# A two-layer attention, convolution and pooling backbone: which of the split operands of attention have 16 bits

## The chip, the cores and the metric

The kernel runs on one core of one Trainium2 chip. The metric is the device time in microseconds of one execution. The kernel before takes 3357.68 us (median of 3 runs, 3351.25 to 3362.43).

## The reference

Two groups of tokens go through two layers: 256 prompt tokens and 2048 sample tokens, each of width 1024. A layer normalizes its input, shifts and scales it, and projects it to queries (8 heads of 64), keys and values (2 heads of 64), gates, and inputs of a short convolution and of a pooling branch. Attention is the part that this case is about:

```
q = rmsnorm(q) * q_g;  k = rmsnorm(k) * k_g          # per head of 64
sample:  q, k = rotary(q), rotary(k);  k, v = [k, cached k], [v, cached v]   # 2048 + 256 keys
s = (q . k) * 64**-0.5
p = softmax(s)
attn = (p . v) * silu(z_a)
out = concat(attn, conv, pool) @ w_out
x = x + gate * out
```

All arrays are float32. The values, keys of the cache and query gains are drawn with a spread eight times the usual one.

## The kernel before, in words

To keep precision the kernel writes each operand of a product as a sum of a high part and a low part, and adds up the products that matter. Most parts have the 32-bit type fp32r, some are f16.

Each layer is two phases. **Phase A** (`phase_a`) loads the input, normalizes it, transposes it, and runs the input projection: per weight chunk, per block of 512 tokens, three products for each of 8 slices of the contraction (lines 477 to 479 and 638 to 640). What comes out goes to scratch arrays in device memory: queries in `q_unit` (high part `qH`, low part `qL`, and a rounded f16 copy `qB`), keys in `put_k` (`kH` and the f16 low part `kL`), values in `put_v` (`vS`, high and low part side by side, 64 + 64 columns). The stores are collected by `store` and issued on SP's queue by `stores` one step later.

**Phase B** (`phase_b`) is attention and the output projection. A unit is one head of one block of 512 queries (or two heads of the prompt's 256); there are 32 sample units of nine steps and four prompt units of one step in each layer, 292 steps. A step handles 256 keys as two tiles of 128:

- `qk` makes the scores of the two tiles in a PSUM tile of 128 x 1024. For each tile there are two products: line 1163 multiplies `KH` (the key's high part, twice, on the two halves of the partitions) with `T1` (the query's high and low part), and line 1164 multiplies `KL` (the key's low part) with `T2` (the rounded query). Row 64 of `KL` and `T2` carries the maximum that is taken off the scores.
- `expo` runs two exponentials on ScalarE: `P` in f32 (line 1173), and `ph`, the high part (line 1175). GpSimd subtracts `ph` from `P` and gives the f16 low part `pl` (line 1182, through the helper on line 183).
- `pv` multiplies values with probabilities: line 1209 takes the 128 columns of `V` (high and low part) with `ph`, two products a step. Line 1216 takes the values' high part `VH` (64 columns, f16, rounded from `V` by `round_v` on line 1048) with `pl`; these products wait in a list and run at the unit's end, 18 in a row, two by two on the two halves of the array's columns.
- `zsum` sums `P` over keys on VectorE (line 1195), in pieces; GpSimd adds the pieces up.
- `max_pieces` computes the scores of a later unit (line 1123) and VectorE reduces them to a maximum (line 1124), about two pieces a step; `max_a`, `max_b` turn the maximum into row 64 of `T2`.
- `outproj` puts some products of the output projection of the block before (lines 1336 to 1338) into each step. In the first of four blocks there is none.

Every engine works its instructions off in the order in which the program issues them, and the loop over steps (line 1605) is that order. At step 2 it calls `round_v` for both prompt heads and the first sample head group, so ScalarE holds those three casts ahead of step 2's exponentials; the casts of the second group come at step 22. `load_kv` loads keys and values on SP's queue and fills row 64 of `KL` (line 1043); its second part runs for the first group at the end of phase A, for the prompt at step 0 and for the second group at step 8. `load_q1` and `load_q2` load `T1` and `T2` some steps before a unit starts; PSUM holds two score tiles.

`outproj_tail` is the output projection of the last block. Its weights go into buffers that attention no longer needs: `half` uses the second group's key and value tiles, `later` and `final` use the tiles of `P` and (in `final`) of `ph`.

Of the kernel before, what the change touches and what calls it, by code (L numbers as in the profile page):

```python
# [22 lines left out]
NS = 2048  # L23
# [16 lines left out]
V_SCALE = 0.0625  # L40
M_SCALE = 256.0
# [55 lines left out]
def hybrid_step(ctx: ExitStack, tc: tile.TileContext, A, O):  # L97
# [25 lines left out]
    qB = [scratch(f"qB{p}", [128, NS], F16) for p in range(4)]  # L123
    qHp = [scratch(f"qHp{p}", [128, NP], F32) for p in range(4)]
    qLp = [scratch(f"qLp{p}", [128, NP], F32) for p in range(4)]
    qBp = [scratch(f"qBp{p}", [128, NP], F16) for p in range(4)]
# [3 lines left out]
    kLp = scratch("kLp", [128, NP], F16)  # L130
    vS = scratch("vS", [128, 18, 2, 128], F32)
    vSp = scratch("vSp", [128, 2, 2, 128], F32)
# [58 lines left out]
    def setup(tp, ptr):  # L191
# [14 lines left out]
        nc.vector.memset(lift, P_LOG2 * float(np.log(2.0)) * 8.0 / M_SCALE)  # L206
# [63 lines left out]
    def phase_a(l, xs_src, xp_src, nxt):  # L270


        with ExitStack() as st, ExitStack() as left:
# [261 lines left out]
            def q_unit(w, b, pair, c):  # L535
# [8 lines left out]
                def post(pair, q):  # L544
# [11 lines left out]
                    qb = w2("qb").bitcast(F16)[:, 0:512].rearrange("p (a n) -> p a n", a=2)  # L556
                    nc.scalar.copy(out=qb, in_=tr)
                    t0 = b.t0 + pair * 256
                    for hp in range(2):
                        dh, dl, db = (qHp, qLp, qBp) if b.prompt else (qH, qL, qB)  # L560
# [9 lines left out]
            def put_v(vsrc, dst):  # L570
                v = w2("vs", F32R)
# [7 lines left out]
            def put_k(k, dh, dl):  # L579
# [4 lines left out]
                lo = w1("kl").bitcast(F16)[:, 0:256]  # L584
                nc.scalar.copy(out=h[:, 0:256], in_=tr)
                nc.vector.tensor_tensor(out=lo, in0=tr, in1=h[:, 0:256], op=ALU.subtract)
                store(dh, h[:, 0:256])
                store(dl, lo)
# [415 lines left out]
    def phase_b(l, xs_src, xp_src, xs_dst, xp_dst, nxt):  # L1004
# [3 lines left out]
        with ExitStack() as st, ExitStack() as left:  # L1008
# [6 lines left out]
            def kv_tiles(prompt):  # L1015
                if prompt:
                    t = wk.tile([128, 4, 512], F32R, tag="cl", name="kvp", bufs=1)
                    vh = wk.tile([128, 2, 2, 64], F16, tag="VHp", name="VHp", bufs=1)
                    for g in range(2):
                        for a, v in zip(kvs[True], (t[:, g, 0:256], t[0:65, g, 256:384].bitcast(F16),  # L1020
                                                    t[:, 2 + g, 0:256].rearrange("p (t e) -> p t e", e=128), vh[:, g])):
                            a.append(v)
# [4 lines left out]
                low = p.tile([128, n + n // 2], F16, tag=f"L{g}", name="L")  # L1027
                for a, t in zip(kvs[False], (p.tile([128, n], F32R, tag=f"KH{g}", name="KH"), low[0:65, 0:n],
                                             p.tile([128, n // 128, 128], F32R, tag=f"V{g}", name="V"),
                                             low[:, n:].rearrange("p (t e) -> p t e", e=64))):  # L1030
                    a.append(t)

            def load_kv(prompt, g, first=True, second=True):
                KH, KL, V, VH = kvs[prompt]
# [6 lines left out]
                if second:  # L1041
                    nc.sync.dma_start(out=KL[g][0:64, 0:n], in_=sl[r, :])
# [7 lines left out]
            kvs = {False: ([], [], [], []), True: ([], [], [], [])}  # L1050
# [10 lines left out]
            def make_unit(prompt, blk, h):  # L1061
# [5 lines left out]
                u.KH, u.KL, u.V, u.VH = kvs[prompt]  # L1067
# [22 lines left out]
            def load_q2(u):  # L1090
                sb = qBp if u.prompt else qB
                u.T2 = lk.tile([65, 512], F16, tag="T2", name="T2", bufs=3)
                for r, ts, c in q_parts(u):
                    nc.sync.dma_start(out=u.T2[0:64, c], in_=sb[u.pair][r, ts])
# [55 lines left out]
            def max_b(u):  # L1150
                ps = borrow["ps"]() if borrow else pmx.tile([128, 512], F32, tag="mx", name="mxb")
                nc.tensor.matmul(out=ps, lhsT=ones_r, rhs=u.dg)
                nc.scalar.activation(out=u.T2[64:65, :], in_=ps[64:65, :], func=AF.Identity, bias=lift[64:65, :],
                                     scale=1.0 / M_SCALE)

# [565 lines left out]
```

## Time and profile before

| | us |
|---|---|
| median of 3 runs | 3357.68 |
| the profiled execution | 3371.42 |
| its span, first to last instruction | 3369.6 |
| busy: PE / VectorE / GpSimd / ScalarE | 3138.9 / 2446.6 / 2125.9 / 1845.8 |

The trace belongs to the profiled execution, which is 13.7 us longer than the median. Phase A of the two layers lies at about 0 to 715 us and 1640 to 2320 us of the span, phase B at about 720 to 1640 us and 2330 to 3370 us. TensorE's work is shown as two engines: PE for the products and PEld for loading their stationary operands. The recorded time of one product is longer than the distance to the next one, since products overlap in the array; the distance between starts says what a product costs.

### The profile page before, as it was taken

Reading aid. Unit: us, or ns where it says so; the run is one execution under the profiler, and the core shown is the slowest. Engines: PE = TensorE matmul, PEld = TensorE weight load, DVE = VectorE, ACT = ScalarE, POOL = GpSimd, SP = SyncE. Lnnn points to the kernel's source line nnn. Section 1 sums busy time; section 2 is a strip of 40 time slices with the busy share of each in tenths; the row PEclk is TensorE's granted clock in tenths of the full one; section 3 lists DMA queues with packets and bytes.
Section 4 is the critical chain, followed back from the end, with each engine's and each line's share of the span. In section 5 each row is a group of like instructions: output and inputs, shape, how many; then the busy total and the mean of one; then the engine's idle time right before and its main releaser. Section 6 shows DMA issues by size and latency. Waiting matters only on the chain. (4 is left out here: it accounts for less than half of the span.)

```text
span 3369.6 us, 48369 instructions
## 1 busy us (share of the span) xinstructions
PE 3138.9 (93%) x17818; PEld 2369.1 (70%) x17818; DVE 2446.6 (73%) x3860; ACT 1845.8 (55%) x2654; POOL 2125.9 (63%) x1192
## 2 busy tenths in 40 slices
PE   6899999988999999999999999999889899998998
PEld 4788888754566666667788787887456566665667
DVE  6546474458888888888466536635898988999885
ACT  3232333248777777777433323323787677776772
POOL 3325352238998898888453435322798888887883
PEclk9999999999999999999999999999899999999999
DMA  7246645350241323133523555334113324232245
GB/s 240 79 151 197 222 131 160 128 130 23 89 144 49 97 74 97 56 114 118 203 85 117 180 181 167 113 103 114 50 54 119 123 60 128 74 111 85 76 138 197
DMA packets 377380, 402.66 MB, mean 119 GB/s; under 512 B 21940, under 2 KB 329144, under 8 KB 376632
## 3 DMA queue, kind: packets, MB, share of 16 engines
q1 hardware_dynamic: 377144, 399.56, 38.3%
q8 instruction: 142, 2.33, 0.3%
q14 instruction: 94, 0.77, 0.1%
HBM read 278.09 MB, written 121.39 MB: 119 GB/s over the span
## 5 line engine op out<-in xcount | busy, mean ns | idle before, releaser
L183 POOL TENSOR_TENSOR pl<-P,ph 128x1024 f16<-128x1024 f32 (+2 forms) x594 | 1401.4, 2379 | 242.3 <-ACT ph L1175 223.2
L1124 DVE TENSOR_REDUCE mr<-mx 128x1 f32<-128x512 f32 x1024 | 693.9, 683 | 214.5 <-PE mx L1123 210.2
L1173 ACT ACTIVATE P<-st 128x1024 f32<-128x1024 f32 x576 | 635.1, 1103 | 324.9 <-PE st L1164 313.8
L1195 DVE TENSOR_REDUCE Z<-P 128x152 f32<-128x912 f32 (+2 forms) x576 | 695.4, 1208 | 13.5 <-ACT P L1173 12.6
L1175 ACT ACTIVATE ph<-st 128x1024 fp32r<-128x1024 f32 x584 | 592.2, 1014 | 0.0
L1123 PE MATMUL mx<-KH,T 128*128 128x512 f32 x1024 | 507.7, 496 | 56.8 <-DVE mr L1124 38.1
L1163 PE MATMUL st<-T,KH 128*128 128x512 f32 x1152 | 506.0, 498 | 9.6 <-ACT ph L1175 9.6
L638 PE MATMUL rest<-xh,wh 128*128 128x512 f32 (+1 forms) x1280 | 486.1, 380 | 1.9 <-ACT wh L428 1.5
L640 PE MATMUL rest<-xh,wl 128*128 128x512 f32 (+1 forms) x1280 | 476.7, 372 | 6.7 <-DVE wl L430 4.9
L639 PE MATMUL rest<-xl,wh 128*128 128x512 f32 (+1 forms) x1280 | 476.8, 372 | 0.8 <-POOL xl L183 0.8
L1164 PE MATMUL st<-T,L 65*128 65x512 f16 x1152 | 459.4, 399 | 0.0
L1209 PE MATMUL pv<-ph,V 128*128 128x512 f32 x1152 | 385.5, 416 | 11.5 <-DVE o L1228 11.5
L1164 PEld LDWEIGHTS <-L 65*128 65x128 f16 x1152 | 113.7, 99 | 302.7 <-issue 301.8
L1123 PEld LDWEIGHTS mx<-KH,T 128*128 128x128 f32 x1024 | 200.3, 196 | 169.7 <-DVE mr L1124 104.8
L430 POOL TENSOR_TENSOR wl<-wf,wh 128x512 fp32r<-128x512 f32 x88 | 121.9, 1386 | 300.5 <-ACT wh L428 285.1
L640 PEld LDWEIGHTS rest<-xh,wl 128*128 128x128 f32 x1280 | 244.1, 191 | 50.5 <-DVE wl L430 5.9
L638 PEld LDWEIGHTS rest<-xh,wh 128*128 128x128 f32 x1280 | 244.9, 191 | 47.2 <-issue 6.3
L639 PEld LDWEIGHTS rest<-xl,wh 128*128 128x128 f32 x1280 | 244.8, 191 | 38.5 <-POOL xl L183 1.2
L477 PE MATMUL qkv<-wh,xh 128*128 128x256 f32 x864 | 252.2, 292 | 3.1 <-ACT wh L428 3.1
L478 PE MATMUL qkv<-wl,xh 128*128 128x256 f32 x864 | 248.8, 288 | 5.3 <-DVE wl L430 2.8
L1163 PEld LDWEIGHTS st<-T,KH 128*128 128x128 f32 x1152 | 229.8, 200 | 26.4 <-ACT ph L1175 12.7
L479 PE MATMUL qkv<-wh,xl 128*128 128x256 f32 x864 | 247.9, 287 | 0.0
(231 smaller groups left out, 5833.0 us busy)
## 6 DMA issues: line engine op xcount, KB each, us to landing
wo<-woH SPq DMA_DIRECT2D x68, 512.0 KB
wo<-woL SPq DMA_DIRECT2D x68, 512.0 KB
wf<-in_w_in SPq DMA_DIRECT2D x50, 512.0 KB
wa<-in_w_ada SPq DMA_DIRECT2D x24, 1024.0 KB
wf<-in_w_in SPq DMA_DIRECT2D x19, 1024.0 KB
woH<-wgh SPq DMA_DIRECT2D x64, 256.0 KB
woL<-wgl SPq DMA_DIRECT2D x64, 256.0 KB
xS<-ox SPq DMA_DIRECT2D x24, 512.0 KB
```

The lines of the kernel that those rows point to most:

```text
L183: nc.gpsimd.tensor_tensor(out=out, in0=a, in1=b, op=op)
L638: nc.tensor.matmul(out=ps[:, 0:b.n], lhsT=wh[:, k, ms], rhs=b.h[:, k, :], start=(k == 0), stop=False)
L639: nc.tensor.matmul(out=ps[:, 0:b.n], lhsT=wh[:, k, ms], rhs=b.l[:, k, :], start=False, stop=False)
L640: nc.tensor.matmul(out=ps[:, 0:b.n], lhsT=wl[:, k, ms], rhs=b.h[:, k, :], start=False, stop=(k == KD - 1))
L1123: nc.tensor.matmul(out=ps, lhsT=u.T1[:, q * 128:(q + 1) * 128], rhs=u.KH[u.g][:, c * 512:(c + 1) * 512])
L1124: nc.vector.reduce_max(out=mr[:, q, c:c + 1], in_=ps, axis=AX.X)
L1163: nc.tensor.matmul(out=ps[:, i, :], lhsT=u.KH[u.g][:, kt], rhs=u.T1, start=True, stop=False)
L1164: nc.tensor.matmul(out=ps[:, i, :], lhsT=u.KL[u.g][0:65, kt], rhs=u.T2, start=False, stop=True)
L1173: nc.scalar.activation(out=P, in_=ps, func=AF.Exp, scale=0.125)
L1175: nc.scalar.activation(out=ph, in_=ps, func=AF.Exp, scale=0.125)
L1195: nc.vector.tensor_reduce(out=z[:, c], in_=u.P[grp][:, 0:ns, c, :].rearrange("p s n t -> p n s t"), axis=AX.XY, op=ALU.add)
L1209: nc.tensor.matmul(out=u.po, lhsT=u.V[u.g][:, 2 * j + i, :], rhs=ph[:, i, :], start=(j == 0 and i == 0), stop=False)
```

## The change

The low score product (line 1164) gets 32-bit operands: `kL` and its tile are fp32r, and `T2` is loaded from `qH` instead of from the rounded copy. The copy `qB`, its cast and its stores are gone. The product of values and probabilities (line 1209) gets 16-bit operands: `vS` holds an f16 high part and an f16 low part, and `ph` is f16. The values' high part that line 1216 uses is now the first 64 columns of `V`, so `VH` and `round_v` are gone. The two scale factors that kept f16 in range are 1 now (`V_SCALE`) or gone (`M_SCALE`). Row 64 of `KL` is filled by a copy of a one instead of a memset. In the tail, `final` can't use the smaller `ph` tiles any more, and half of one weight part is loaded by `later`.

```
-V_SCALE = 0.0625
-M_SCALE = 256.0
+V_SCALE = 1.0
...
-    qB = [scratch(f"qB{p}", [128, NS], F16) for p in range(4)]
-    kL = scratch("kL", [128, NS + NC], F16)
+    kL = scratch("kL", [128, NS + NC], F32)
-    vS = scratch("vS", [128, 18, 2, 128], F32)
+    vS = scratch("vS", [128, 18, 2, 128], F16)
...
-                    qb = w2("qb").bitcast(F16)[:, 0:512].rearrange("p (a n) -> p a n", a=2)
-                    nc.scalar.copy(out=qb, in_=tr)
...
-                        store(db[2 * c + hp][:, t0:t0 + 256], qb[:, hp, :])
...
-                v = w2("vs", F32R)
+                v = w2("vs").bitcast(F16)[:, 0:512]
...
-                lo = w1("kl").bitcast(F16)[:, 0:256]
+                lo = w1("kl", F32R)
...
-                low = p.tile([128, n + n // 2], F16, tag=f"L{g}", name="L")
-                for a, t in zip(kvs[False], (p.tile([128, n], F32R, tag=f"KH{g}", name="KH"), low[0:65, 0:n],
-                                             p.tile([128, n // 128, 128], F32R, tag=f"V{g}", name="V"),
-                                             low[:, n:].rearrange("p (t e) -> p t e", e=64))):
+                for a, t in zip(kvs[False], (p.tile([128, n], F32R, tag=f"KH{g}", name="KH"),
+                                             p.tile([65, n], F32R, tag=f"KL{g}", name="KL"),
+                                             p.tile([128, n // 128, 128], F16, tag=f"V{g}", name="V"))):
...
-                    nc.vector.memset(KL[g][64:65, 0:n], M_SCALE)
-                    load(V[g], sv[:, :, g, :])
-
-            def round_v(prompt, g):
-                V, VH = kvs[prompt][2:]
-                nc.scalar.copy(out=VH[g], in_=V[g][:, :, 0:64])
...
+                    nc.vector.tensor_copy(out=KL[g][64:65, 0:n], in_=ones1[64:65, 0:1].to_broadcast([1, n]))
+                    nc.sync.dma_start(out=V[g], in_=sv[:, :, g, :])
...
-                u.T2 = lk.tile([65, 512], F16, tag="T2", name="T2", bufs=3)
+                u.T2 = lk.tile([65, 512], F32R, tag="T2", name="T2", bufs=3)
...
-                ph = wk.tile([128, 2, 512], F32R, tag="ph", name="ph", bufs=LAG)
+                ph = wk.tile([128, 2, 512], F16, tag="ph", name="ph", bufs=LAG)
...
-                        nc.tensor.matmul(out=u.po[64 * i:64 * i + 64], lhsT=u.VH[u.g][:, 2 * j + i, :], rhs=pl[:, i, :],
+                        nc.tensor.matmul(out=u.po[64 * i:64 * i + 64], lhsT=u.V[u.g][:, 2 * j + i, 0:64], rhs=pl[:, i, :],
...
                 def later():
-                    load_w(2, 1, wk.tile([128, KD, 256], F32R, tag="P", name="wt", bufs=2), 0)
+                    w = wk.tile([128, 12, 256], F32R, tag="P", name="wt", bufs=2)
+                    load_w(2, 1, w[:, 0:8], 0)
+                    load_w(3, 1, w[:, 8:12], 4)
                     load_x(1, "ox", D, 2)
...
                 def final():
-                    for k0 in (4, 0):
-                        load_w(3, 1, wk.tile([128, 4, 256], F32R, tag="ph", name="wt", bufs=LAG), k0)
-                    load_w(3, 0, wk.tile([128, KD, 256], F32R, tag="P", name="wt", bufs=2), 0)
+                    w = wk.tile([128, 12, 256], F32R, tag="P", name="wt", bufs=2)
+                    load_w(3, 1, w[:, 8:12], 0)
+                    load_w(3, 0, w[:, 0:8], 0)
...
-                if s == 2:
-                    for g in range(2):
-                        round_v(True, g)
-                    round_v(False, 0)
...
-                if s == PR['rv1']:
-                    round_v(False, 1)
```

## Rows read from the trace of the kernel before

**Rows 1.** Stretches: us, busy us of each engine (instructions), granted clock, DMA share, GB/s.

```profile
100.00:715.00 615.00, 588.55 (x3545) 504.97 (x3544) 326.28 (x660) 181.31 (x335) 212.28 (x178) 0.98 0.50 155
720.00:1000.00 280.00, 251.39 (x1253) 154.82 (x1251) 240.88 (x325) 220.38 (x289) 241.92 (x114) 0.97 0.31 89
1000.00:1600.00 600.00, 583.60 (x3287) 404.57 (x3286) 516.24 (x698) 439.37 (x537) 527.03 (x243) 0.99 0.29 88
2600.00:3280.00 680.00, 637.89 (x3483) 433.93 (x3482) 615.38 (x814) 489.41 (x670) 564.08 (x260) 0.97 0.33 100
727.00:736.00 9.00, 5.68 (x18) 3.50 (x16) 5.67 (x7) 7.11 (x8) 6.48 (x4) 0.62 0.64 168
```

**Rows 2.** Waits of PE, 2600 to 3280 us: total us, times, longest us.

```profile
PE mx L1123 <- DVE mr L1124: 22.7, 38, 2.6
```

**Rows 3.** Timeline of ScalarE and PE, start of layer 0's attention: start, us, engine, instruction.

```profile
727.39 0.30 ACT L1048 CAST VHp<-kvp 128x128 f16<-128x128 f32 x1 [1.90 <-DMA kvp<-vSp]
728.65 1.06 ACT L1173 ACTIVATE P<-st 128x1024 f32<-128x1024 f32 x1
...
726.02 0.39 PE L1164 MATMUL st<-T,L 65*128 65x512 f16 x1
730.66 0.80 PE L1163 MATMUL st<-T,KH 128*128 128x512 f32 x1 [3.32 <-ACT ph L1175]
```

**Rows 4.** Timeline of SP's queue and PE there: the prompt's last query load.

```profile
727.35 0.59 SPq L180 DMA_DIRECT2D T<-qLp  x1
732.23 0.99 PE L1130 MATMUL mx<-kvp,T 128*128 128x256 f32 x2
```

**Rows 5.** Timeline of PE in phase A: the first and the last of 27 products.

```profile
299.98 0.40 PE L638 MATMUL rest<-xh,wh 128*128 128x512 f32 x1
305.88 0.39 PE L640 MATMUL rest<-xh,wl 128*128 128x512 f32 x1
```

**Rows 6.** Timeline of PE in one dense step of attention.

```profile
1030.72 0.63 PE L1209 MATMUL pv<-ph,V 128*128 128x512 f32 x2
1031.42 0.39 PE L1163 MATMUL st<-T,KH 128*128 128x512 f32 x1
1031.65 0.39 PE L1164 MATMUL st<-T,L 65*128 65x512 f16 x1
1032.12 0.39 PE L1164 MATMUL st<-T,L 65*128 65x512 f16 x1
```

**Rows 7.** Timeline of PE at a unit's end, and the durations of line 1216 (min/median/max).

```profile
1019.21 0.63 PE L1209 MATMUL pv<-ph,V 128*128 128x512 f32 x2
1019.77 2.13 PE L1216 MATMUL pv<-pl,L 128*64 128x512 f16 x18
...
L1216 PE MATMUL pv<-pl,L x1152: 376/379/637, 754.2 to 3313.8; 128*64 128x512 f16 x192
```

**Rows 8.** Timeline of PEld (weight loads) in that dense step.

```profile
1031.65 0.10 PEld L1164 LDWEIGHTS <-L 65*128 65x128 f16 x1 [0.27 <-issue]
```

**Rows 9.** Groups of GpSimd by form: busy us, mean ns | idle before and releasers.

```profile
L183 POOL TENSOR_TENSOR pl<-P,ph 128x1024 f16<-128x1024 f32 x558 | 1361.8, 2459 | 237.3 <-ACT ph L1175 218.3 <-PE mx L1123 13.6 <-PE pv L1209 1.7
L183 POOL TENSOR_TENSOR Z<-Z 128x512 f32<-128x512 f32 x128 | 166.7, 1303 | 99.9 <-DVE Z L1195 86.4 <-PE st L1164 7.2 <-PE pv L1216 2.5
L183 POOL TENSOR_TENSOR ml<-po,mh 128x1032 fp32r<-128x1032 f32 x4 | 11.9, 2972 | 25.4 <-ACT mh L656 25.4
```

**Rows 10.** Groups of ScalarE: the casts of the queries.

```profile
L557 ACT CAST qb<-trq 128x512 f16<-128x512 f32 x36 | 21.1, 585 | 141.8 <-DVE ql L555 132.7 <-POOL ra L183 9.1
L554 ACT CAST qh<-trq 128x512 fp32r<-128x512 f32 x36 | 20.8, 577 | 12.1 <-DVE sq L517 4.9 <-DVE nt_v L156 2.5 <-DMA qB<-qb 2.4
```

**Rows 11.** Groups of VectorE: the memset of row 64, and two products of 512 columns.

```profile
L1043 DVE MEMSET L<- 1x2304 f16 x4 | 7.9, 1978 | 8.9 <-DMA mH<-mh 7.3 <-issue 1.6
L1279 DVE TENSOR_TENSOR mixl<-o,mixh 128x512 fp32r<-128x512 f32 (+1 forms) x40 | 77.8, 1946 | 3.4 <-ACT mixh L1274 3.4
L1267 DVE TENSOR_TENSOR o<-o,rlb 128x512 f32<-128x512 f32 (+1 forms) x40 | 25.0, 624 | 10.5 <-PE rlb L1266 10.4
```

More of the change, by code (lines that the diff above doesn't have):

```diff
@@ L205, in setup @@
         nc.vector.memset(vones_h, V_SCALE)
-        nc.vector.memset(lift, P_LOG2 * float(np.log(2.0)) * 8.0 / M_SCALE)
+        nc.vector.memset(lift, P_LOG2 * float(np.log(2.0)) * 8.0)
         nc.vector.memset(sT, 0.0)
@@ L1017, in kv_tiles @@
                     t = wk.tile([128, 4, 512], F32R, tag="cl", name="kvp", bufs=1)
-                    vh = wk.tile([128, 2, 2, 64], F16, tag="VHp", name="VHp", bufs=1)
                     for g in range(2):
-                        for a, v in zip(kvs[True], (t[:, g, 0:256], t[0:65, g, 256:384].bitcast(F16),
-                                                    t[:, 2 + g, 0:256].rearrange("p (t e) -> p t e", e=128), vh[:, g])):
+                        for a, v in zip(kvs[True], (t[:, g, 0:256], t[0:65, g, 256:512], t[:, 2 + g, 0:128]
+                                                    .bitcast(F16).rearrange("p (t e) -> p t e", e=128))):
                             a.append(v)
@@ L1041, in load_kv @@
                 if second:
-                    nc.sync.dma_start(out=KL[g][0:64, 0:n], in_=sl[r, :])
-                    nc.vector.memset(KL[g][64:65, 0:n], M_SCALE)
-                    load(V[g], sv[:, :, g, :])
-            def round_v(prompt, g):
-                V, VH = kvs[prompt][2:]
-                nc.scalar.copy(out=VH[g], in_=V[g][:, :, 0:64])
-            kvs = {False: ([], [], [], []), True: ([], [], [], [])}
+                    load(KL[g][0:64, 0:n], sl[r, :])
+                    nc.vector.tensor_copy(out=KL[g][64:65, 0:n], in_=ones1[64:65, 0:1].to_broadcast([1, n]))
+                    nc.sync.dma_start(out=V[g], in_=sv[:, :, g, :])
+            kvs = {False: ([], [], []), True: ([], [], [])}
             kv_tiles(False)
@@ L1066, in make_unit @@
                 u.nst = 1 if prompt else 9
-                u.KH, u.KL, u.V, u.VH = kvs[prompt]
+                u.KH, u.KL, u.V = kvs[prompt]
                 u.g = h // 4
@@ L1090, in load_q2 @@
             def load_q2(u):
-                sb = qBp if u.prompt else qB
-                u.T2 = lk.tile([65, 512], F16, tag="T2", name="T2", bufs=3)
+                sh = qHp if u.prompt else qH
+                u.T2 = lk.tile([65, 512], F32R, tag="T2", name="T2", bufs=3)
                 for r, ts, c in q_parts(u):
-                    nc.sync.dma_start(out=u.T2[0:64, c], in_=sb[u.pair][r, ts])
+                    load(u.T2[0:64, c], sh[u.pair][r, ts])
             def load_z(u):
@@ L1152, in max_b @@
                 nc.tensor.matmul(out=ps, lhsT=ones_r, rhs=u.dg)
-                nc.scalar.activation(out=u.T2[64:65, :], in_=ps[64:65, :], func=AF.Identity, bias=lift[64:65, :],
-                                     scale=1.0 / M_SCALE)
+                nc.scalar.activation(out=u.T2[64:65, :], in_=ps[64:65, :], func=AF.Identity, bias=lift[64:65, :])
             GRP = 3
```

15 lines of the change are left out of this document (7 added, 8 removed).

## The prediction

> **What bounds the kernel now.** I read the stretches first, then the waits of PE, then the timelines of PE, PEld and ScalarE, and last the groups by form. In phase A TensorE is the bound: PE is busy 588.55 of 615 us, ScalarE 181.31 [rows 1]. In attention's blocks 2 to 4 of layer 0 PE is busy 583.60 of 600 us, with GpSimd at 527.03 and VectorE at 516.24; in the same blocks of layer 1 it is 637.89 of 680, with VectorE at 615.38 [rows 1], and there PE waits 22.7 us for VectorE's maxima alone [rows 2]. In the first block (720 to 1000 us) nobody is full: PE 251.39 of 280, GpSimd 241.92, VectorE 240.88 [rows 1]. So the reader is to see a kernel in which PE ends last, with two engines 5 to 12 points behind it: a saving on PE is passed on nearly whole in layer 0's dense blocks, about half in layer 1's, a third in first blocks. Weighted by steps (216, 216 and 144 of 576 sample steps, shares 0.9, 0.5, 0.3) I pass on 0.6.
>
> **Part 1, the casts of `round_v`.** At step 2 of layer 0, ScalarE has its three casts ahead of the exponentials and sits 1.90 us idle for the second prompt value to land. The scores of step 2 were through at about 726.02 + 0.39 = 726.41, but `P` starts at 728.65: 2.24 us late. PE then waits 3.32 us [rows 3], and after that pause the granted clock is down: 0.62 on average over 727 to 736 us, against 0.99 in the dense blocks [rows 1], so it is at the lower of its two levels, 1.2 GHz, for much of that time. Without the casts the pause shrinks from 3.7 to about 1.5 us. If the clock still falls, the gain is 2.24 us; if it doesn't, up to half of the 5.3 us from 730.66 to 736 is saved too, and it is about 5. What is late next is the prompt's query: its last load is issued until 727.94, and the maximum of line 1130 needs it, at 732.23 today and about 730.0 then [rows 4]. The load has 2 us to land in; so there is room for 2.2 us and little more, and I take 3 per layer. Layer 1 starts in the same way, so 6 us, between 4 and 10. The cast at step 22 lies beside a ScalarE that is busy 439.37 of 600 us [rows 1]: nothing.
>
> **Part 2, the products on PE.** One fp32r product of 512 columns costs (305.88 - 299.98) / 26 = 227 ns from start to start in phase A [rows 5]. In attention it costs more: from `pv` at 1030.72 to `st` at 1031.42 lie three, 233 ns each [rows 6]. A pair of line 1164 and line 1163 costs 1032.12 - 1031.65 = 470 ns by the printed digits, and the f16 product follows the fp32r one by 230 [rows 6]: f16 behind fp32r costs about what fp32r costs, 225 to 240. Only f16 behind f16 is cheaper: the 18 of line 1216 are nine pairs side by side, and (2130 - 379) / 8 = 219 ns lie between pairs [rows 7].
>
> - `pv`: two fp32r (466 ns) become two f16: the first behind fp32r, about 228, the second behind f16, 219, less what the first pair's start costs in that figure, 216. That is 22 ns less a step, 576 x 22 = 12.7 us. Bounds: 0 if f16 is no cheaper here, 2 x 17 x 576 = 20 us if both run at 216.
> - `KL`: an f16 between fp32r becomes fp32r. From -6 ns (phase A's 227 instead of 233) to +10; I take +6, for two a step 12 x 576 = 6.9 us more (-7 to +12). Its weight load, 0.10 us now [rows 8], gets longer, but fp32r loads run under the product before, as phase A's cadence of 227 shows.
> - the unit's end: from `pv` at 1019.21 to line 1216 at 1019.77 are 560 ns, where two products cost 466; some 95 ns are lost at the change from fp32r to f16 of 64 columns [rows 7]. If the type makes that gap it goes (64 units x 0.1 = 6.4 us); if the change to half columns makes it, it stays. I take half, 3.2.
>
> Together 12.7 - 6.9 + 3.2 = 9.0 us, passed on at 0.6: 5.4 us (-7 to +18 before passing on).
>
> The Trainium skill, "TensorE: Matmul & The Clock Gate" (Back-to-back issue gap), gives N / 2.4 + 2.5 ns for a warm product whatever its type: 216 ns at 512. By that rule alone part 2 is nothing, and the sum below would be 7.5 us. The f16 rows agree (219 with the first pair in it), the fp32r rows don't (227 and 233), and the measurement decides; the rule is in the second rival.
>
> **Part 3, the engines beside PE.** `ph` as f16: ScalarE's two casts from one PSUM tile take 585 ns to f16 and 577 to fp32r [rows 10], so the 584 exponentials gain or lose some 16 ns each, under 10 us on an engine that is a quarter idle: 0. GpSimd's subtraction then reads one 16-bit operand, which no row shows. What it writes makes no difference (2459 ns for 1024 columns to f16, 1303 for 512 to f32, so a slope per column that fits both), and I take 2.46 us unchanged; nearest rows on either side are 1303 and 2972 ns [rows 9]. It has slack: GpSimd is busy 88% of the dense blocks, so up to some 13% more hides, and a faster one gains nothing while PE is the bound.
>
> **Part 4, phase A.** 36 casts `qb` (21.1 us) and 72 stores go. The cast also makes ScalarE sit 141.8 us, mostly for VectorE's subtraction of the same tile [rows 10], with weight casts behind it. But PE waits little there: 615 - 588.55 = 26.5 us in layer 0, most of it for VectorE. I take 3 us, 0 to 10. Fewer stores help SP's queue, which nothing on PE waits for there.
>
> **Part 5, loads and row 64.** `T2` and `KL` double in bytes, `V` halves; `T2` is loaded five steps (15 us) before its unit, like `T1`, whose loads have the size `T2` gets. Nothing. The copy into row 64 replaces a memset of 1978 ns [rows 11]; from 0 to as much again. VectorE operations with two SBUF operands suffer beside GpSimd: 1946 ns against 624 for one with a PSUM operand and the same 512 columns [rows 11]. If the copy suffers so too it waits for one subtraction, up to 2.46 us, at two long copies in phase B and four short ones. I take 1.5 us more in all (0 to 10).
>
> The Trainium skill, "SBUF — State Buffer" (SBUF: two separate sides), says that VectorE's two-port operations, fp32 copies from SBUF to SBUF among them, and GpSimd's instructions lock each other out for a whole instruction. By it each copy in phase B pays what I have as the upper end; without it, nothing. The rows on the two products agree with a lock; none shows a copy.
>
> The tail moves 0.5 MB from `final` to `later`, before its use; the tail's waits are on `cl`, loaded earlier. Nothing, 2 us either way.
>
> **Sum**, against the profiled execution's 3371.42 us (span 3369.6 and 1.8 around it): -6 - 5.4 - 3 + 1.5 = -12.9, so 3358.5. The median of the runs shown is 13.7 us under that execution; the same change from 3357.68 gives 3345.
>
> **Rivals.**
> 1. The gain is absorbed (chance 0.31). PE's term is nothing, by the skill's rule or because `KL` gives back what `pv` saves; the other terms are -6 - 3 + 1.5 = -7.5, or 3350, and with VectorE and GpSimd taking more, up to 3357. For it: every f16 product between fp32r ones costs as much as fp32r. Against it: PE's own pause at step 2 is not hidden by anything.
> 2. The other side: the values' weight load shows (0.09). An f16 load starts only when the product before it is through (line 1164's load starts at 1031.65, with its product; its idle is put down to "issue") [rows 8], and at the unit's end 95 ns are lost in just such a load [rows 7]. If `V` with 128 rows behaves like that one and not like line 1164's, each step pays 0.1 us in front of `pv`: (100 + 12) x 576 = 64.5, passed on 0.6, 39 us, less 6 and 3, plus 1.5: +31, or 3389. It decides from about 40 ns a step. Against it: line 1164's load has as many columns, 128, and shows no gap.
> 3. GpSimd's mixed subtraction is slower (0.05). At 2972 ns, nine per unit add 4.6 us to the 9 x 2.459 + 2 x 1.303 + 0.65 = 25.4 us of GpSimd per unit, which makes 30. A unit takes about 29 (527.03 / 25.4 = 20.7 units in the 600 us [rows 1]), so GpSimd would be full at +1 us a unit, and with some idle time left +1.4: 64 x 1.4 = 90, or 3450. It decides from 13%. No row of a 16-bit operand speaks for it.
>
> **How the numbers follow.** The forecast has 0.55. A measurement of this kernel can't tell a change under 0.3%, 10 us, from none. Faster by more: 0.55, the forecast with its better half of bounds; within: 0.31; slower: 0.14, rivals 2 and 3. All good ends together (-10, 0.9 x 18, -10) make -36, 3321, and I go to 3320; upwards the bounds of the forecast and part of rival 2 reach 3366. The forecast's own range is 3325 to 3350.
>
> **What would show it.** Right: no casts of line 1048 and a pause of PE under 2 us at step 2; starts of line 1209's pairs nearer to 445 than 466 ns; line 1164 at 230 to 240; GpSimd's subtraction within 2% of 2.46 us. Wrong: a gap ahead of line 1209 in each step, a subtraction over 2.7 us, a unit's length that stays at its old value, a new wait on row 64 or on the prompt's loads.

## The result: 44 us faster, three times the forecast and more

The changed kernel takes 3311.22 us (median of 4 runs, 3305.09 to 3318.36), the one before 3355.03 (3351.25 to 3362.43): a ratio of 0.9864 with the 95% interval 0.9838 to 0.9889, where 3345 was forecast and 3320 the lower end. The profiled executions have spans of 3311.0 and 3369.6 us.

The page of the changed kernel, busy time by engine: PE works 21.6 us less than before, GpSimd 153.7, ScalarE 24.2.

```profile
PE 3117.3 (94%) x17818; PEld 2457.1 (74%) x17818; DVE 2439.7 (74%) x3860; ACT 1821.6 (55%) x2610; POOL 1972.2 (60%) x1192
```

Its stretches, in the columns of [rows 1] (the second to fourth are the first block, the dense blocks of layer 0 and those of layer 1):

```profile
100.00:711.00 611.00, 589.93 (x3557) 506.08 (x3556) 331.64 (x661) 172.64 (x319) 213.40 (x179) 0.98 0.49 151
720.00:1000.00 280.00, 256.68 (x1298) 175.06 (x1296) 246.74 (x334) 221.99 (x294) 226.94 (x118) 0.97 0.33 96
1000.00:1600.00 600.00, 586.52 (x3360) 442.59 (x3360) 516.69 (x699) 449.17 (x548) 485.69 (x250) 1.00 0.30 88
2600.00:3250.00 650.00, 613.24 (x3370) 454.69 (x3368) 575.17 (x779) 472.78 (x645) 492.66 (x258) 0.97 0.34 103
```

GpSimd in the dense blocks fell from 527.03 to 485.69 us of 600. Its subtraction is why, and with it VectorE's `mixl` fell ([rows 9] and [rows 11]); the copy into row 64 costs about what the memset did, and PE's waits for VectorE's maxima in layer 1's dense blocks are halved, 22.7 us [rows 2] to 12.1 (over the whole traces they fall from 38.1 to 33.7 only):

```profile
L180 POOL TENSOR_TENSOR pl<-P,ph 128x1024 f16<-128x1024 f32 x558 | 1211.6, 2183 | 319.0 <-ACT ph L1162 295.7 <-PE mx L1111 11.6 <-PE st L1151 4.7
...
L1266 DVE TENSOR_TENSOR mixl<-o,mixh 128x512 fp32r<-128x512 f32 (+1 forms) x40 | 68.7, 1717 | 3.0 <-ACT mixh L1261 3.0
L1035 DVE CAST KL<-ones 1x2304 fp32r<-1x2304 f32 x4 | 8.2, 2044 | 6.9 <-DMA mL<-ml 6.8
...
PE mx L1111 <- DVE mr L1112: 12.1, 20, 1.9
```

Two timelines answer to [rows 3] and [rows 7]. Where ScalarE's casts stood, `P` starts 2.73 us after the one ahead of it, and between 720 and 733 us PE waits 0.43 us at the longest, for a query's load. At a unit's end the low products start 0.54 us after the last pair, 0.56 before: the pair is shorter, the gap of some 0.1 us at the change to half columns is still there.

```profile
724.97 1.17 ACT L1160 ACTIVATE P<-st 128x1024 f32<-128x1024 f32 x1
727.70 1.09 ACT L1160 ACTIVATE P<-st 128x1024 f32<-128x1024 f32 x1 [0.66 <-PE st L1151]
...
726.25 0.48 PE L1118 MATMUL mx<-kvp,T 128*128 128x256 f32 x2 [0.43 <-DMA T<-qLp]
...
1036.57 0.61 PE L1196 MATMUL pv<-ph,V 128*128 128x512 f16 x2
1037.11 0.84 PE L1203 MATMUL pv<-pl,V 128*64 128x512 f16 x6
```

The first of a unit's low products marks its end, and these 64 marks cut every trace into the same six stages (us; "units" are 32 in a layer, the first eight follow the projections):

| kernel (span) | to first mark | layer 0 attention | to layer 1's first mark | layer 1, eight units | layer 1, the other 23 | after the last |
|---|---|---|---|---|---|---|
| before (3369.6) | 754.2 | 890.7 | 726.9 | 243.4 | 695.8 | 58.6 |
| c_before (3361.9) | 755.8 | 887.2 | 724.1 | 242.0 | 694.7 | 58.1 |
| changed (3311.0) | 744.7 | 879.3 | 703.6 | 235.9 | 688.2 | 59.3 |
| a_qb (3345.4) | 747.0 | 891.8 | 720.5 | 240.1 | 687.3 | 58.8 |
| b_qbfirst (3353.7) | 750.9 | 891.6 | 713.1 | 243.4 | 696.5 | 58.2 |
| b_split (3325.3) | 756.6 | 880.7 | 727.3 | 238.1 | 664.4 | 58.3 |
| a_split (3284.8) | 737.9 | 882.4 | 701.8 | 241.4 | 661.7 | 59.6 |
| a_pool (3280.2) | 735.5 | 874.7 | 702.1 | 243.9 | 664.8 | 59.2 |

The largest drop, some 20 us, lies in layer 1's projections; the rest is spread over attention and the start. The first column also varies by some 10 us between kernels that do the same there. Each row is one execution: that of a_qb lies 15 us above its median, that of b_qbfirst 14.

### The profile page after: what moved, and what is told of

Read it like the earlier page. It is cut to its first block, busy times and chain, and to the rows that moved or that the text cites. A ratio compares the mean times of both kernels' runs of the same rounds, so it can differ in the third digit from the quotient of the medians.

```text
span 3311.0 us, 48199 instructions
## 1 busy us (share of the span) xinstructions
PE 3117.3 (94%) x17818; PEld 2457.1 (74%) x17818; DVE 2439.7 (74%) x3860; ACT 1821.6 (55%) x2610; POOL 1972.2 (60%) x1192
## 5 line engine op out<-in xcount | busy, mean ns | idle before, releaser
L180 POOL TENSOR_TENSOR pl<-P,ph 128x1024 f16<-128x1024 f32 (+2 forms) x594 | 1247.5, 2113 | 325.3 <-ACT ph L1162 301.4
L1162 ACT ACTIVATE ph<-st 128x1024 f16<-128x1024 f32 x584 | 591.8, 1013 | 0.0
L1111 PE MATMUL mx<-KH,T 128*128 128x512 f32 x1024 | 494.1, 483 | 46.7 <-DVE mr L1112 33.7
L1150 PE MATMUL st<-T,KH 128*128 128x512 f32 x1152 | 466.8, 405 | 3.1 <-ACT ph L1162 3.1
L1151 PE MATMUL st<-T,KL 65*128 65x512 f32 x1152 | 464.2, 403 | 0.0
L1196 PE MATMUL pv<-ph,V 128*128 128x512 f16 x1152 | 357.8, 393 | 8.8 <-DVE o L1215 6.1
L1151 PEld LDWEIGHTS st<-T,KL 65*128 65x128 f32 x1152 | 221.8, 193 | 48.8
L1150 PEld LDWEIGHTS st<-T,KH 128*128 128x128 f32 x1152 | 222.6, 193 | 42.9 <-ACT ph L1162 6.1
L180 POOL TENSOR_TENSOR Z<-Z 128x512 f32<-128x512 f32 x128 | 166.5, 1300 | 136.6 <-DVE Z L1182 110.9
```

The costliest lines, as they stand in the source:

```text
L180: nc.gpsimd.tensor_tensor(out=out, in0=a, in1=b, op=op)
L1111: nc.tensor.matmul(out=ps, lhsT=u.T1[:, q * 128:(q + 1) * 128], rhs=u.KH[u.g][:, c * 512:(c + 1) * 512])
L1150: nc.tensor.matmul(out=ps[:, i, :], lhsT=u.KH[u.g][:, kt], rhs=u.T1, start=True, stop=False)
L1151: nc.tensor.matmul(out=ps[:, i, :], lhsT=u.KL[u.g][0:65, kt], rhs=u.T2, start=False, stop=True)
L1162: nc.scalar.activation(out=ph, in_=ps, func=AF.Exp, scale=0.125)
L1196: nc.tensor.matmul(out=u.po, lhsT=u.V[u.g][:, 2 * j + i, :], rhs=ph[:, i, :], start=(j == 0 and i == 0), stop=False)
```

## The experiments

Each label beginning with "a" edits the changed kernel, with "b" the one before. All ratios are to the kernel before, with their 95% intervals.

**c_before** has no edit.

> The kernel before, unchanged, for a second trace of it: same, 3355 us within 0.3%. Theory 1 (ScalarE's in-order stalls) expects PE's pauses in the query units of layer 1's phase A and at step 2 to be there again, about 17 us and 2 x 5.6 us; if they are an accident of the first trace, they are gone here and theory 1 falls.

3357.23 us, 0.9996 (0.9975 to 1.0017). The long first units and the 724.1 us of layer 1's projections come back, so they belong to the kernel.

**a_qb: the query cast alone put back.**

```
+                    qb = w2("qb").bitcast(F16)[:, 0:512].rearrange("p (a n) -> p a n", a=2)
+                    nc.scalar.copy(out=qb, in_=tr)
...
+                        store(db[2 * c + hp][:, t0:t0 + 256], qb[:, hp, :])
```

> The kernel after with the f16 cast of the queries and its stores put back; nothing reads the copy. Theory 1: most of phase A's gain goes, +15 to +20 us on 3311, so 3326 to 3331. Rival (my prediction's part 4, the cast is hidden beside PE): +3 us, 3314. Rival 2 (GpSimd's faster subtraction is the gain): +0 to 3.

3332.45 us, 0.9921 (0.9890 to 0.9952): 21 us over the changed kernel (19, give or take 13, by the two intervals). The two traces are 34 us apart, 17 of them in layer 1's projections (703.6 to 720.5) and 12 in layer 0's attention. By the medians nearly half of the gain is this cast.

**b_qbfirst: the cast kept, and issued ahead of VectorE's subtraction.**

```
-                    nc.vector.tensor_tensor(out=lv, in0=tr, in1=hv, op=ALU.subtract)
                     ...
                     nc.scalar.copy(out=qb, in_=tr)
+                    nc.vector.tensor_tensor(out=lv, in0=tr, in1=hv, op=ALU.subtract)
```

> The kernel before with two lines of the projection exchanged: ScalarE's 16-bit cast of the query is issued ahead of VectorE's subtraction that makes the 32-bit low part; no work is taken away, the stores stay. Theory 1 (what the cast cost is its wait for VectorE at the head of ScalarE's order, which held back weight casts in layer 1's projections): ScalarE's idle time ahead of the cast falls from 141.8 us to under 60, the projections of layer 1 fall from 727 towards 705 us, 3334 to 3342 in all. Rival (it is the cast's own work and its eight stores of each unit that cost): the idle time may fall, the time stays at 3350 to 3358.

3341.82 us, 0.9957 (0.9941 to 0.9973): 14 us less without any work taken away. The cast's group (idle time ahead of it after the second bar) stood at 141.8 us in [rows 10]:

```profile
L556 ACT CAST qb<-trq 128x512 f16<-128x512 f32 x36 | 21.2, 588 | 29.5 <-DVE sq L517 19.2 <-DMA qB<-qb 8.8 <-POOL ra L183 0.7
```

So the wait was the larger part: 14 us (9 to 20) of the 21. How it looks before, in ScalarE's timeline in layer 1's projections: the next tile's high cast is done at 1804.17, then ScalarE stands for 7.70 us until VectorE's `ql`, with everything behind it.

```profile
1803.59 0.58 ACT L554 CAST qh<-trq 128x512 fp32r<-128x512 f32 x1 [1.85 <-POOL ra L183]
1811.87 0.58 ACT L557 CAST qb<-trq 128x512 f16<-128x512 f32 x1 [7.70 <-DVE ql L555]
```

PE's idle time in that stage (the stretch less its busy time), before and then in the changed kernel, is 39.4 and 24.9 us. Its busy time falls as well, by 10.6 us for nearly the same products, at a granted clock of 0.99 in place of 0.98:

```profile
1650.00:2360.00 710.00, 670.63 (x3960) 588.51 (x3959) 392.85 (x761) 234.11 (x425) 264.95 (x215) 0.98 0.45 140
```

```profile
1630.00:2315.00 685.00, 660.08 (x3951) 581.72 (x3950) 399.65 (x760) 221.83 (x400) 263.68 (x214) 0.99 0.44 138
```

**a_rv: the three value casts at step 2 put back, unread.**

```
+                if s == 2:
...
+                    for g in range(2):
+                        nc.scalar.copy(out=vhp[:, g], in_=kvs[True][2][g][:, :, 0:64])
+                    nc.scalar.copy(out=vh, in_=kvs[False][2][0][:, :, 0:64])
```

> The kernel after with ScalarE's three casts of values put back at step 2, into tiles that nothing reads. Theory 1: the pause at the start of attention comes back in both layers, +9 to +12 us, 3320 to 3323. My prediction's part 1 says +6, 3317. If later idle time absorbs the pause: +0 to 3.

3319.14 us, 0.9885 (0.9857 to 0.9914): 8 us over the changed kernel, which the two intervals don't set apart from none. The pause itself is plain: the timeline shows what [rows 3] showed, ScalarE waiting for the second prompt value and PE waiting for ScalarE:

```profile
718.26 0.30 ACT L1602 COPY VHp<-kvp 128x128 f16<-128x128 f16 x1 [1.70 <-DMA kvp<-vSp]
...
721.53 0.79 PE L1150 MATMUL st<-T,KH 128*128 128x512 f32 x1 [3.11 <-ACT ph L1162]
```

**b_pv: only the 16-bit values and high part; low score products and query cast as before.**

```
-                ph = wk.tile([128, 2, 512], F32R, tag="ph", name="ph", bufs=LAG)
+                ph = wk.tile([128, 2, 512], F16, tag="ph", name="ph", bufs=LAG)
...
-            def round_v(prompt, g):
```

> The kernel before with only the 16-bit pairs for the values and for the probabilities' high part (the casts for the low product go with them); the score products' low operands stay 16-bit, and so does the query cast. It differs from 'a_qb' in the low score products' type alone. Theory 1 (three separate savings: the query cast and its stores some 20 us, the value casts at the start of each layer's attention 7, the products of values and probabilities 22 ns for each of 576 pairs, less what the low score products cost at 32 bits, some 6.9): casts 7 and products 12.7 of 3356 give 3337 (3328 to 3345), which is 5 to 7 us less than 'a_qb' should show at the same query cast if the low score products' cost is as read; 'a_qb' measured 3332.5, so theory 1 is strained already and wants 3325 to 3337. Rival A (the prediction's, the step is bound elsewhere and a lighter product is absorbed): 3348 to 3356. Rival B (GpSimd's subtraction, faster with a 16-bit operand, carries the gain in attention): mean of the 1024-column subtraction near 2183 ns, attention of layer 1 at or under 716 us, 3325 to 3340; 'b_pool16' must then show the larger part of it.

3332.19 us, 0.9925 (0.9910 to 0.9941), the same as a_qb. Apart from the tail's weight loads the two differ in the low score products' operands alone (their type, their loads, row 64), so those are worth nothing that these runs can tell (each interval is 10 to 20 us wide).

**a_pool: 46 columns of each subtraction done twice.**

```
                     padd(pl, P, ph, ALU.subtract)
+                    padd(pl[:, 1, 466:512], P[:, 1, 466:512], ph[:, 1, 466:512], ALU.subtract)
```

> The kernel after, with the last 46 columns of each subtraction done twice on GpSimd, which adds about 0.28 us and so gives back what the subtraction had gained (2.46 to 2.18 us). Theory 1: GpSimd had slack in any case, +0 to +5 us, 3311 to 3316. Rival 2 (the attention part of the gain is GpSimd's): +15 to +20 us, 3326 to 3331.

3276.58 us, 0.9756 (0.9730 to 0.9782): 35 us *under* the changed kernel, with more work on GpSimd (2126.1 us). Both theories fell here: that GpSimd has slack (0 to 5 us more), and that its shorter subtraction is the gain (15 to 20 more). What had changed beside GpSimd was VectorE: its `mixl` needs 1251 ns in the mean, where the changed kernel has 1717. So a third theory: some of VectorE's operations on SBUF operands stand still until an instruction of GpSimd ends, and a boundary between two lets them in.

**a_split: the subtraction in two halves, no column twice.**

```
-                    padd(pl, P, ph, ALU.subtract)
+                    for i in range(2):
+                        padd(pl[:, i], P[:, i], ph[:, i], ALU.subtract)
```

> The changed kernel with GpSimd's subtraction issued as two instructions of 512 columns in place of one of 1024; no work is added but a second start. Theory 3 (VectorE's additions and mixes with two operands in SBUF are held until GpSimd's instruction ends, so that a boundary between two lets VectorE in; this is why 'a_pool', with more GpSimd work in two instructions, was 35 us faster than the changed kernel): VectorE's mixes fall from a mean of 1.72 us towards 1.2, blocks 2 to 4 of layer 1 from 716 to about 693 us, and the time to 3275 to 3285. Rival (the extra time itself spreads the steps, a slower low part does it): the subtraction's sum stays within 0.1 us of 2183 ns, nothing is spread, and the time stays at 3306 to 3320. Theory 1 (GpSimd is no bound): 3306 to 3316.

3284.86 us, 0.9785 (0.9766 to 0.9803), as the third theory had it, though GpSimd works 80 us more (2051.8). One place shows the mechanism, VectorE above and GpSimd below, first in the changed kernel:

```profile
2566.59 2.10 DVE L156 TENSOR_SCALAR nt_y<-nt_t 128x2 int32<-128x2 int32 x1
2568.60 0.68 DVE L1112 TENSOR_REDUCE mr<-mx 128x1 f32<-128x512 f32 x1
...
2566.27 2.39 POOL L180 TENSOR_TENSOR pl<-P,ph 128x1024 f16<-128x1024 f32 x1 [0.57 <-ACT ph L1162]
...
2569.33 0.79 PE L1111 MATMUL mx<-KH,T 128*128 128x512 f32 x1 [2.17 <-DVE mr L1112]
...
2569.00:2573.00 4.00, 3.67 (x9) 2.06 (x10) 4.00 (x7) 1.13 (x2) 1.84 (x2) 0.51 1.10 341
```

An operation on two columns takes 2.10 us: it ends at 2568.69, and GpSimd's subtraction, under way when it began, at 2568.66. The maximum `mr` behind it on VectorE is late, PE waits 2.17 us for that, and then the granted clock is 0.51, its lower level, for the next 4 us (the last line). Here the wait is paid about twice: 2.17 us, and by estimate some 2 more in those 4 us. In a_split the same operation is let in at the boundary between the halves (two from 2566.45 in 2.30 us); PE waits 1.06 us, and the clock of the same stretch stays up:

```profile
2566.53 1.12 DVE L156 TENSOR_SCALAR nt_y<-nt_t 128x2 int32<-128x2 int32 x1
...
2566.45 2.30 POOL L180 TENSOR_TENSOR pl<-P,ph 128x512 f16<-128x512 f32 x2 [0.40 <-ACT ph L1162]
...
2568.30 0.50 PE L1111 MATMUL mx<-KH,T 128*128 128x512 f32 x1 [1.06 <-DVE mr L1112]
...
2569.00:2573.00 4.00, 3.06 (x14) 1.51 (x13) 4.00 (x6) 2.03 (x3) 2.87 (x3) 1.00 1.09 342
```

Layer 1's last 23 units, in the changed kernel and then in a_split: the same 3535 products take PE 17.5 us less, at a granted clock of 0.99 in place of 0.96, and its idle time falls by 9 us. In these two traces the shorter pauses gave back more by the clock than by themselves.

```profile
2563.43:3251.67 688.24, 647.36 (x3535) 478.49 (x3535) 610.12 (x827) 497.00 (x676) 520.77 (x274) 0.96 0.35 105
...
2563.50:3225.18 661.68, 629.85 (x3535) 466.59 (x3534) 587.58 (x825) 496.79 (x676) 548.42 (x472) 0.99 0.36 109
```

The Trainium skill, "SBUF — State Buffer" (SBUF: two separate sides), has VectorE (with two SBUF inputs, or in a two-port mode) and GpSimd share one port pair under an exclusive lock, held for a whole instruction. The rows above agree with it. The row below, also of a_split, goes further: one `mixl` stood through six instructions of GpSimd that followed each other without a pause, so a boundary does not always let VectorE in.

```profile
1196.35 7.54 DVE L1267 TENSOR_TENSOR mixl<-o,mixh 128x512 fp32r<-128x512 f32 x1
...
1196.65 6.70 POOL L180 TENSOR_TENSOR pl<-P,ph 128x512 f16<-128x512 f32 x6
```

**b_split: the same two halves in the kernel before.**

> The kernel before, with each subtraction on GpSimd issued as two instructions of 512 columns; nothing of the change. Theory 3 (VectorE is held until GpSimd's instruction ends, in the kernel before as well, and PE waits for what is queued behind on VectorE): mean of the mixes from 1.95 towards 1.25 us, blocks 2 to 4 of layer 1 from 695 to about 670 us, 3326 to 3340 in all, though GpSimd works some 100 us more. Rival (the gain of the split belongs to the changed kernel, where GpSimd has more idle time): 3350 to 3370.

3327.26 us, 0.9908 (0.9892 to 0.9924): 29 us from this alone, 31 in layer 1's last 23 units (695.8 to 664.4). The lock cost the kernel before, too.

```profile
L1280 DVE TENSOR_TENSOR mixl<-o,mixh 128x512 fp32r<-128x512 f32 (+1 forms) x40 | 35.7, 893 | 4.3 <-ACT mixh L1275 4.2
```

**a_split4: four quarters.**

```
-                    padd(pl, P, ph, ALU.subtract)
+                    for i in range(2):
+                        for c in range(0, 512, 256):
+                            q = slice(c, c + 256)
+                            padd(pl[:, i, q], P[:, i, q], ph[:, i, q], ALU.subtract)
```

> The changed kernel with the subtraction in four instructions of 256 columns. From 2183 ns for one of 1024 and twice 1188 ns for 512 the four come to some 2.75 us a step of about 3.3 us. Theory 3: VectorE is held no longer than some 0.7 us at a time, its mixes fall from the 1.24 us of 'a_split' towards 1.0 us, and the time to 3268 to 3282. Rival (VectorE gets in only where GpSimd pauses, as in the one mix of 7.54 us beside five subtractions in 'a_split'; with GpSimd busier there are fewer pauses): mixes of several us return, 3290 to 3310.

3328.19 us, 0.9911 (0.9895 to 0.9928): the rival holds, and worse than it said. Quarters follow each other so closely that VectorE is shut out for many of them; the row-64 copy stood 7.81 us beside the last 11 of a run of 14, and PE's waits for `mr` (us, times, longest), 33.7 us in 52 in the changed kernel, grow:

```profile
2334.76 7.81 DVE L1035 CAST KL<-ones 1x2304 fp32r<-1x2304 f32 x1
...
2332.50 8.86 POOL L180 TENSOR_TENSOR pl<-P,ph 128x256 f16<-128x256 f32 x14
...
PE mx L1111 <- DVE mr L1112: 58.7, 47, 7.1
```

**a_cut: 896 and 128 columns.**

```
-                    padd(pl, P, ph, ALU.subtract)
+                    for q in (slice(0, 448), slice(448, 512)):
+                        padd(pl[:, :, q], P[:, :, q], ph[:, :, q], ALU.subtract)
```

> The changed kernel with the subtraction cut into 896 and 128 columns, no column done twice. Theory 3 (a short second instruction opens a boundary at little cost, and adds too little to keep GpSimd busy through several steps): VectorE's mixes near 1.25 us and no pause of PE over 4 us behind them, 3268 to 3282, at or under 'a_pool' (3276.6) and 'a_split' (3284.9). Rival (it was the added 0.28 us of work that spread the steps in 'a_pool'): 3290 to 3311.

3287.80 us, 0.9786 (0.9761 to 0.9811): the boundary alone gives what a_split gave. The time is some 6 us above what was expected of it, `mixl` stays at 1584 ns, and why a_pool is 8 to 11 us better than both is not settled (the intervals overlap).

**a_mixp: a_split with `mixl` computed by GpSimd.**

```
-                    nc.vector.tensor_tensor(out=lo[:, 0:n], in0=o[:, 0:n], in1=h[:, 0:n], op=ALU.subtract)
+                    padd(lo[:, 0:n], o[:, 0:n], h[:, 0:n], ALU.subtract)
```

> 'a_split', with the output's low part (the mix, o less its high part) computed by GpSimd in place of VectorE. Theory 3 (VectorE's own work beside GpSimd is what holds PE): VectorE loses 49.5 us of mixes, the one of 7.54 us behind which PE paused 5.8 us among them, GpSimd gains some 42 us; 3262 to 3278. Rival (on GpSimd the mix comes late behind the subtractions, and the output projection waits for it): PE's waits ahead of the low output products grow, 3285 to 3300.

3284.32 us, 0.9787 (0.9769 to 0.9805), no better than a_split. The pause at 1199 us is gone, but two others come, each behind an operation of four columns that stood beside a run of GpSimd's instructions, as this one; the mix is not the only operation that can be shut out.

```profile
3018.44 7.42 DVE L150 SCALAR_TENSOR_TENSOR nt_t<-nt_y 128x4 f32<-128x4 f32 x1
```

**b_pool16: GpSimd reads the upper 16 bits of the 32-bit high part, in place.** It leaves the lower bits of the high part out of the low part.

```
+                    ph16 = ph.rearrange("p a n -> p (a n)").bitcast(mybir.dt.bfloat16)...
+                    padd(pl, P, ph16[:, :, :, 1], ALU.subtract)
```

> The kernel before, but GpSimd's subtraction reads only the upper 16 bits of each high part, in place (so it leaves the lower bits of the high part out of the low part); all else as before. Theory 1 (PE and ScalarE carry the gain, a faster GpSimd is worth nothing while PE is the bound): the subtraction may fall from 2459 ns, the time stays at 3350 to 3358. Rival B (GpSimd's subtraction and what VectorE waits for beside it): the subtraction falls towards 2183 ns, and the time by 10 to 20 us, to 3336 to 3346. If the subtraction stays at 2459 ns, its speed-up in the changed kernel came from the operand's stride and not from its 16 bits, and the time stays.

The subtraction stays at 2459 ns and the time at 3359.90 us, 1.0012 (0.9997 to 1.0028). With a stride of 4 bytes a 16-bit operand gains nothing; what this says of a faster subtraction is nothing.

**a_stride: the 16-bit high part at a stride of 4 bytes.**

```
-                ph = wk.tile([128, 2, 512], F16, tag="ph", name="ph", bufs=LAG)
+                ph = wk.tile([128, 2, 512, 2], F16, tag="ph", name="ph", bufs=LAG)[:, :, :, 0]
```

> The changed kernel, but the 16-bit high part lies in memory with a stride of 4 bytes (every second 16-bit place of its tile is left empty), as the 32-bit one did; ScalarE writes and PE and GpSimd read it through that stride, nothing else changes. 'b_pool16', which read 16 bits at a stride of 4 bytes, kept GpSimd's subtraction at 2459 ns, so it should go back from 2183 to about 2459 ns here. Theory 3 (a shorter subtraction lets VectorE go sooner and this is a part of the changed kernel's gain): VectorE's mixes go back from a mean of 1.72 towards 1.95 us, and the time to 3318 to 3328. Rival (all of the gain in attention is PE's lighter products of values and probabilities): 3307 to 3315. If the interval between two products of values and probabilities leaves 216 ns, the stride costs PE too, and that part (576 pairs) is taken off first.

3340.01 us, 0.9951 (0.9934 to 0.9968), 29 us over the changed kernel. The subtraction is back at 2459 ns, but ScalarE's write grew from 1013 to 1325 ns and PE's products of values from a mean of 393 to 400, so three things moved and it decides nothing.

**a_vh and a_kh: the subtraction's second operand is 1024 resident columns of the 16-bit values, or of the 32-bit keys.** The low part is another number in both.

```
+                    padd(pl, P, u.V[u.g][:, 0:8, :]..., ALU.subtract)
...
+                    padd(pl, P, u.KH[u.g][:, 0:1024].bitcast(F32)..., ALU.subtract)
```

> The changed kernel, with GpSimd's subtraction in the image's units taking 1024 columns of the 16-bit values (resident, packed) in place of the high part, so that the low part is another number; the control of 'a_kh'. The subtraction waits for P alone and may start up to 1 us sooner in its step; its duration should stay 2183 ns. Both theories: 3300 to 3320.

> As 'a_vh', but the second operand is 1024 columns of the 32-bit keys (resident, packed), so that the low part is another number; PE, ScalarE and VectorE have the instructions of 'a_vh'. The subtraction should take some 2459 ns (so 276 ns for each of 558). Theory 3 (GpSimd's duration sets how long VectorE is held, and PE waits for VectorE): 6 to 18 us over 'a_vh', with longer mixes on VectorE. Rival (the prediction's: a GpSimd off the bound costs nothing, and the whole gain in attention is PE's lighter products): within 3 us of 'a_vh'.

3317.31 us, 0.9869 (0.9847 to 0.9891), and 3334.90 us, 0.9916 (0.9895 to 0.9937): 17.6 us for GpSimd's duration alone, with every other engine's instructions the same. Groups of the two, a_vh and then a_kh:

```profile
L180 POOL TENSOR_TENSOR pl<-P,V 128x1024 f16<-128x1024 f32 x558 | 1208.1, 2183 | 251.8 <-ACT P L1160 250.7
...
PE mx L1111 <- DVE mr L1112: 41.9, 61, 2.1
```

```profile
L180 POOL TENSOR_TENSOR pl<-P,KH 128x1024 f16<-128x1024 f32 x558 | 1359.0, 2458 | 175.6 <-ACT P L1160 135.2 <-DMA kvp<-kHp 38.4
...
PE mx L1111 <- DVE mr L1112: 56.6, 83, 5.1
```

A part of the 17.6 belongs to the two layers' starts, where PE pauses some 4 us longer each in a_kh, behind a row-64 copy of 5.61 and 5.76 us; in layer 0 PE was also 2 us behind before attention began. Without some 9 us for the two starts (5.5 to the first mark and 3.5 between the layers, by the marks of the two traces), 9 are left. So GpSimd's 276 ns a step is worth between 9 and 18 us in this pair. The pair is not the changed kernel, though: its subtraction starts after `P` and not after `ph`, and a_vh spends 712.8 us in layer 1's last 23 units where the changed kernel, with the same duration, spends 688.2. When the subtraction starts matters too.

**The traces together.** Call an operation of VectorE held when it takes 0.3 us and 30% more than the shortest of its kind in the trace. In layer 1's last 23 units there are 36 to 69 of them in each of the 17 traces, and every one ends within its shortest duration and 60 ns of the end of an instruction of GpSimd; of the changed kernel's other operations there a third do. Reductions and operations with a PSUM operand are never among them (`mr` stays between 670 and 694 ns). The largest single share is not `mixl` but `oy`, the final normalization's product of two SBUF operands, of which layer 0 has none: 447 to 2440 ns in the changed kernel.

```profile
L1364 DVE SCALAR_TENSOR_TENSOR oy<-oy,nt_y,fg 128x256 f32<-128x256 f32 x56 | 46.1, 835 | 4.2 <-DMA oy<-xS 4.2
```

What the held operations take above the shortest of their kind, summed, follows the stage's length better than `mixl` alone (us, worked out from the traces). In a_cut, where `mixl` hardly fell, the held time of `oy` did (20.4 to 5.8). a_mixp is the row that fits least.

| kernel | held time | layer 1, the other 23 |
|---|---|---|
| before / c_before | 75.3 / 74.7 | 695.8 / 694.7 |
| b_split | 35.6 | 664.4 |
| changed | 61.2 | 688.2 |
| a_split / a_cut / a_pool | 40.1 / 39.4 / 35.1 | 661.7 / 661.8 / 664.8 |
| a_mixp | 41.8 | 672.0 |
| a_split4 | 47.7 | 680.8 |
| a_vh / a_kh | 84.1 / 95.9 | 712.8 / 716.3 |

## Why the prediction was wrong, by its own steps

The sum was -12.9, the change gave -44. The steps' own experiments add up to it by their medians: the query cast 21, the value casts 8, GpSimd's subtraction 9 to 18, which leaves 6 us or less for PE's products. No run has them together, and each has an interval of its own.

- **Part 4, phase A (3 us, 0 to 10): the first step that failed.** It measured 21. The prediction had the row with 141.8 us of ScalarE's wait and the weight casts behind it, and set it aside because "PE waits little there", with 26.5 us of layer 0. Layer 1's projections, which the prediction never opened, had 39.4 us. The mechanism was named; its size was read in the wrong stage.
- **Part 3, GpSimd ("2.46 us unchanged", "a faster one gains nothing while PE is the bound"): the second.** Both halves fell. The packed 16-bit operand took it to 2183 ns, and that is worth 9 to 18 us by a_kh against a_vh. An engine with 12% of slack was treated as off the path; what it did was hold VectorE, which PE waits for. The prediction had this in hand: its part 5 set 1946 against 624 ns for an operation beside GpSimd [rows 11], and weighed the lock for the new copy only, not for the 40 mixes, the products `oy` and the small operations that were there already.
- **The clock, outside the sum but for part 1.** In the result's four runs the changed kernel's mean granted clock is 0.976 to 0.981, in c_before's twelve 0.971 to 0.978 (middle values 0.979 and 0.974). By estimate the difference of 0.005 is at most some 17 us of 3340, a part of what each step above gave: a pause that goes gives back some of the low clock behind it, and the prediction passed its savings on at 0.6 instead.
- **Part 1, the value casts (6 us, 4 to 10): right as far as is known.** The pause went and came back with the casts; a_rv's 8 us are not clear of the noise.
- **Part 2, PE's products (9.0, passed on 5.4): the two prices right, the sum too high.** A pair's ends lie 233 ns apart before and 216 after (worked out from the traces; 12.7 us forecast, 9.8 by this, as the product ahead costs what it did). A pair of score products lies 464 ns from the next before and 471 after (mean, at the full clock), so the 32-bit low one costs some 7 ns more, 8 us in all (6.9 forecast); b_pv against a_qb shows no difference in time. The 3.2 us for the unit's end did not come: with either type the last pair's end and the first low product's lie 333 ns apart, so the type doesn't make that gap. That leaves some 2 us of the 9.0. Nor do the stated bounds of the three terms (-7 to +18) follow from their own ends, which give -12 to +33.
- **Part 5 and the tail (+1.5, 0): small, as said.** The copy takes 2044 ns for the memset's 1978, and the tail 0.7 us more. That the copy can suffer from the lock is seen in a_split4 and a_kh.
- **Rivals.** None came in the time. Half of rival 1 (the second one, as part 2 calls it) came on PE: `KL` gives back 8 of the 9.8 us that `pv` saves. The absorption did not: VectorE was held for 75 of layer 1's last 696 us, so what looked like full engines was in part the lock. The values' weight load shows nowhere, and GpSimd's mixed subtraction is faster, not slower.
- **The range** reached 3320 with "all good ends together"; part 3 had no good end at all, because a gain on GpSimd had been excluded by a reason ("PE is the bound") that does not exclude it. With its own ends for part 2 the range would have reached some 3308 and held the result, by the wrong term.

The fastest version here is a_pool (0.9756 of before); a_split, a_mixp and a_cut lie 8 to 11 us above it by their medians. Cutting the subtraction in two gives 26 us on top of the change and 29 without it.

## What to carry to other kernels

Read an in-order engine's long wait ahead of a cheap instruction as a cost of everything queued behind it, and look for who needs that in every stage and layer, not in the first one that is at hand. An engine with slack can still set the pace through what it locks: when one of its operations shows three times the duration of its sibling, see which instruction of the neighbour ends at the same moment. Exchanging two lines gave 14 us and cutting one instruction in two 29, against 44 for the retyping with all its edits; no run has the first two together.

## What the runs showed of the hardware that was not expected

- GpSimd's subtraction of 1024 columns takes 2459 ns with a 32-bit second operand, 2183 with a packed 16-bit one, 2459 with a 16-bit one at a stride of 4 bytes. The Trainium skill, "GPSIMD Engine Reference" (Instruction dispatch, the C++ chunk loop), puts some 2.5 cycles on an element for the two reads and names no type there; these rows differ by type.
- VectorE can be shut out beyond one instruction of GpSimd: 7.54 us beside six halves, 7.81 beside eleven quarters. Size is no protection: an operation on two columns took 2.10 us, one on four 7.42.
- A held `oy` of the changed kernel ends 0.28 to 0.29 us after an instruction of GpSimd does, 20 times of 20 (worked out from the trace).
- A 16-bit write at a stride of 4 bytes costs ScalarE 1325 ns instead of 1013 for 1024 columns, and PE's product some 10 ns when it reads it (a pair's ends lie 225 ns apart instead of 216).
